# Modulation channels 5 to 8 as rows on TensorE in the mixer, x scaled during the first loads, plain first feed-forward tiles

## The chip, the cores and the metric

The kernel runs on one core of a Trainium2 chip. TensorE (PE) multiplies, VectorE (DVE), ScalarE (ACT) and GpSimd (POOL) do the element-wise work, and SyncE (SP) issues the transfers between HBM and the on-chip memory. Each engine takes its instructions in the order of one queue, and an instruction that waits holds up those behind it. The metric is device time in microseconds (us), the median of three runs.

## The reference

One layer of a diffusion backbone: a feed-forward block with half weight (FFN1), a token mixer of two parallel groups (gated linear attention, GLA, and a chunked gMLP), a second feed-forward block (FFN2) and a final RMSNorm. It has 1024 latent tokens, 256 context tokens, width 1024, hidden width 2816. Nine modulation channels of 1024 numbers each come from the conditioning vectors: `m_x` for the latents, `m_c` for the context.

```python
def adaln(cond, w, b):                       # w: (1024, 9 * 1024)
    return (jax.nn.silu(cond) @ w + b).reshape(cond.shape[0], ADA_MODS, 1, D_MODEL)

x = x + 0.5 * m_x[:, 2] * swiglu(modulate(rmsnorm(x, norm1_g), m_x[:, 0], m_x[:, 1]), ff1_in, ff1_out)
h = h + 0.5 * m_c[:, 2] * swiglu(modulate(rmsnorm(h, norm1_g), m_c[:, 0], m_c[:, 1]), ff1_in, ff1_out)
y_x = modulate(rmsnorm(x, norm2_g), m_x[:, 3], m_x[:, 4])          # and y_c from h
...                                          # projections, 3x3 grid convolution, GLA scans, gMLP
x = x + m_x[:, 5] * mix_x
x = x + 0.5 * m_x[:, 8] * swiglu(modulate(rmsnorm(x, norm3_g), m_x[:, 6], m_x[:, 7]), ff2_in, ff2_out)
return rmsnorm(x, final_g)
```

Channels 5 to 8 are needed for the latents only: 5 scales the mixer's output, 6 and 7 are the shift and scale in front of FFN2, 8 scales its output.

## The kernel before, in words

Activations are kept transposed: 8 tiles of 128 channels (index `k` or `dt`), and tokens in blocks of 512, 512 (`tb` 0 and 1) and 256 (`tb` 2, the context). A product to full precision is three matmuls, high part by high part, high by low and low by high, for each of its K tiles; the weights' halves `wh`/`wl` (`gh`, `gl`, `vh`, `sh`, ... in the FFNs) come from a `raw` tile by an ACT copy and a subtraction on POOL or DVE.

The FFNs work on 22 hidden tiles. For each, the two 512-token blocks and the two halves of K are combined in the Strassen-Winograd manner: seven products of 12 matmuls with 512 columns instead of eight (84 instead of 96). `winograd` orders the products of a hidden tile 1, 2 | 5, 7, 6 | 3, 4, and puts 1 and 2 of the next tile ahead of 3 and 4 (`first`). FFN1 also has 48 matmuls of 256 columns per hidden tile for the context (`gc`). The right operands (`hl`, seven sums or differences of normalized x, in two halves) are made once per FFN by `right_ops`, on DVE and ACT.

Modulation is computed in two ways. Channels 0 and 1 as rows on PE (`ada_first`): silu(c), two columns wide, is the stationary operand; each 128x1024 tile of the weights `wa` moves through; the 2x512 sums are copied by ACT (`row`, L214) and turned into columns by small matmuls (`cols`, L216). The other seven as dot products on DVE (`ada_part`): for each of 8 tiles and 2 halves a 256 KB load `ar<-in_wb` and an instruction `junk<-ar,cr` (L169) that multiplies by a broadcast silu(c) and accumulates along the row. Channels 2 to 4 (96 loads in the source, both conditions) run in FFN1, 5 to 7 (48 instructions, behind the GLA output of block 1) while the mixer ends, and 8 (16) in FFN2.

The order is not the source's. A scheduler simulates the engines, takes ready instructions by priority, and writes one queue for each engine; `after(a, b)` fixes an order by hand. Tiles come from pools with a set number of buffers by tag: `raw` 2, `ar` 2, `w` 6, `m` 8, `d` 32, `h` 7, PSUM banks `pg` and `po` 3 each, `pn` 2. A load into a pool waits until the last reader of the buffer's previous tile is done. `load` puts a 512 KB piece into `raw` unless a tag is given.

In the mixer, `mixer_front` projects K, then the four value tiles ("v tiles", `z` by L357, L359, L360: 60 matmuls), evacuates them by ACT (`acc`, `ct`, L813), convolves them on DVE (L791) and transposes them (`tr`, L841), then the two query tiles. At the mixer's end `wo_half`/`wo_add` multiply with the output projection; DVE adds to x (L1372), and x comes back from HBM (`x<-xd`, L1317).

Of the kernel before, what the change touches and what calls it, by code (L numbers as in the profile page):

```python
# [26 lines left out]
class Layer:  # L27
# [150 lines left out]
    def cond_row(self, j, c, dst):  # L178

        nc = self.nc  # L180
        n = c.stop - c.start
        t = self.tile(self.sb, 512, "ar", "cv")[:, :n] if n <= 512 else dst
        nc.sync.dma_start(t, self.a["cvec"][j:j + 1, c].to_broadcast([P, n]))
        nc.scalar.activation(dst, t, AF.Silu)
# [18 lines left out]
    def ada_rows(self, src, pr, i):  # L203
        wt = self.load(src[i], tag="d")
        for h in range(2):
            self.nc.tensor.matmul(pr[h][:2], self.sc[:, i, :], wt[:, h * 512:h * 512 + 512],  # L206
                                  start=(i == 0), stop=(i == NK - 1))

    def ada_cols(self, ch, pr):
        nc = self.nc  # L210
        row = self.m("row")
        pt = self.po("cols")
        for h in range(2):
            nc.scalar.activation(row[:2, h * 512:h * 512 + 512], pr[h][:2], AF.Copy)  # L214
            for dt in range(4 * h, 4 * h + 4):
                nc.tensor.matmul(pt[:, 2 * dt:2 * dt + 2], row[:2, dt * P:(dt + 1) * P], self.ident[:2, :2],  # L216
                                 start=True, stop=True)
        self.ada_bias(ch, 2, pt[:, :2 * NK].rearrange("p (k j) -> p k j", j=2))

    def ada_first(self):  # L220

        pr = [[self.po("row") for _ in range(2)], [self.pg("row") for _ in range(2)]]
        for i in range(NK):
            for ch in range(2):
                self.ada_rows(self.a["wa"][ch], pr[ch], i)
        for ch in (1, 0):
            self.ada_cols(ch, pr[ch])
# [56 lines left out]
    def spread(self, y, nt):  # L284

        nc = self.nc
        bc = self.pn("bc")
        for t in range(nt):
            nc.tensor.matmul(bc[:, t * P:(t + 1) * P], y[:, t:t + 1].to_broadcast([P, P]), self.ident,
                             start=True, stop=True)  # L290
        return bc
# [154 lines left out]

    def right_ops(self, tb, coef, bc, mov):
# [3 lines left out]
        for k in (0, 4, 1, 5, 2, 6, 3, 7):  # L451
# [4 lines left out]
        def out(i, b, k):  # L456
            t = self.hl(b)
            mov[i][k] = t[:, :512], t[:, 512:]

        for k in range(4):  # L460
            if tb == 0:
                out(1, self.x[k][0], k)
                out(2, self.x[k + 4][0], k)
            else:
                (b11, b12), (b21, b22) = self.x[k][:2], self.x[k + 4][:2]
                self.combos(b11, b12, b21, b22, lambda i, b: out(i, b, k))
# [14 lines left out]
    def winograd(self, jobs):  # L481
# [24 lines left out]

        first(0)
        for j, job in enumerate(jobs):
# [11 lines left out]
    def ffn(self, mov, yc, w1, w2, gates, load_x, load_c, tail, done, after_out=None):  # L520
# [14 lines left out]
        def plain(ps, parts, moving):  # L535

            n = len(parts)
            for i, ((hi, lo, c), (mh, ml)) in enumerate(zip(parts, moving)):
                nc.tensor.matmul(ps, hi[:, c], mh, start=i == 0, stop=False)  # L539
                nc.tensor.matmul(ps, hi[:, c], ml, start=False, stop=False)  # L540
                nc.tensor.matmul(ps, lo[:, c], mh, start=False, stop=i == n - 1)  # L541

        class Hidden:
# [3 lines left out]
            def ctx(s, i):  # L547
                w = s.w()
                rows = [(*w[r], slice(k * P, k * P + P)) for r in ((1, 2), (0, 4))[i] for k in range(4)]
# [3 lines left out]
                plain(ps, rows, yc)  # L553
# [9 lines left out]
                nc.sync.dma_start(hc[s.f // 2, :, h:h + 512], o.bitcast(F32))  # L563

# [51 lines left out]
        for f in range(NF):  # L616
            w = lazy(w1[f], nc.vector)
            jobs.append((w, 0, mov, Hidden(f, w)))
# [9 lines left out]
        class Out:  # L628
# [4 lines left out]
            def ctx(s):  # L633
                w = s.w()
                ps = layer.po("oc")
                for i in range(2):
                    rows = [(*w[r], slice(s.col + k * P, s.col + k * P + P)) for r in ((1, 2), (0, 4))[i]
                            for k in range(s.kd)]
                    plain(ps[:, i * 256:i * 256 + 256], rows, s.right()["ctx"])
# [62 lines left out]
        def last():  # L702
# [3 lines left out]
                     for i in range(2)]  # L706
            rows = lambda w, i, col: [(*w[r], slice(col + k * P, col + k * P + P)) for r in ((1, 2), (0, 4))[i]
                                      for k in range(kd)]
            for tb in range(2):
# [6 lines left out]
                for m, i, w, col in tiles:  # L716
                    dt = m + 4 * i
                    ps = self.po("o") if i else self.pg("o")
                    plain(ps, rows(w, i, col), right)
# [8 lines left out]
            if yc:  # L728
# [6 lines left out]
                for m, i, w, col in tiles:  # L735
# [4 lines left out]
                    plain(ps, rows(w, i, col), right)  # L740
# [33 lines left out]
        self.winograd(jobs)  # L774
# [188 lines left out]
    def mixer_front(self, y):  # L963
# [356 lines left out]
    def mixer(self, y, done=None):  # L1320
# [8 lines left out]
        row = self.d("cr")  # L1329
        self.cond_row(0, slice(0, 1024), row)  # L1330
        for ch in (5, 6, 7):
            for h in range(2):
                for dt in range(NK):
# [210 lines left out]
```

## Time and profile before

| | us |
|---|---|
| median of 3 runs | 2159.13 (2155.48 to 2160.04) |
| the profiled execution | 2155.53 |
| its span, first to last instruction | 2153.8 |
| PE busy, DVE busy | 2015.6, 1503.2 |
| mean granted clock of PE | 0.968 of 2.4 GHz |

In the span's order: the start up to about 130 us, FFN1 to about 860, the mixer's front to 1094, GLA and gMLP to 1316, the output projection to about 1452, FFN2 to the end. A row of a timeline gives start and duration in us, the engine, the line of the kernel, what is written from what, how many instructions it groups, and in brackets the idle time of the engine before it with its releaser. Durations of pipelined matmuls overlap: twelve of 512 columns stand in 2.88 us though each has 0.39.

### The profile page before, as it was taken

What the parts mean: (1) busy time and instruction counts of PE and PEld (TensorE: products, weight loads), DVE (VectorE), ACT (ScalarE), POOL (GpSimd) and SP (SyncE); (2) the same over time, 40 slices, a digit from 0 to 9 for tenths busy, and PEclk for the clock granted to TensorE, in tenths of its full rate; (3) what the DMA queues carried; (4) which work ended last, traced back from release to release, by engine and by line L of the source; (5) the groups of instructions that cost most, each with busy time, mean ns of one, the idle gap of its engine ahead of it and who ended that gap; (6) DMA issues with size and microseconds to landing.
All of it is one profiled execution on the core that took longest, in us unless ns stands there. A gap on an engine that the chain in (4) does not pass through costs nothing.

```text
span 2153.8 us, 28445 instructions
## 1 busy us (share of the span) xinstructions
PE 2015.6 (94%) x10868; PEld 1669.6 (78%) x10868; DVE 1503.2 (70%) x2503; ACT 816.5 (38%) x1297; POOL 379.9 (18%) x215
## 2 busy tenths in 40 slices
PE   6799999999999999898999998787999999999997
PEld 1678888888887888787788877565888888868875
DVE  3976665656655779869888377778677786755585
ACT  3643333333333121256456345325343444442111
POOL 0000000000025555223210010300000000065740
PEclk9799999999999999999999899897999999999998
DMA  7033333333368786321111126550444343458742
GB/s 286 25 127 118 123 142 118 122 118 118 118 222 340 275 295 240 147 79 54 49 56 50 35 91 219 200 183 28 166 158 165 112 181 137 182 216 350 306 143 79
DMA packets 111273, 332.27 MB, mean 154 GB/s; under 512 B 12448, under 2 KB 15392, under 8 KB 111136
## 3 DMA queue, kind: packets, MB, share of 16 engines
q1 hardware_dynamic: 111136, 330.45, 41.8%
q8 instruction: 85, 1.39, 0.3%
q14 instruction: 52, 0.43, 0.1%
HBM read 231.31 MB, written 99.09 MB: 153 GB/s over the span
## 4 chain that ended last, share of the span: by engine, by line
PE 72%; DVE 18%; DMA 5%; issue 2%; ACT 2%; POOL 0%; SPq 0%; DVEq 0%; ACTq 0%
PE c L492 14%; PE a L492 14%; PE f L492 14%; PE b L492 7%; DVE acc L791 3%; DMA ar<-in_wb 2%; PE gc L541 2%; PE gc L540 2%; PE gc L539 2%; PE row L206 1%; DVE hl L444 1%; PE o L541 1%; PE o L539 1%; PE o L540 1%; DVE junk L169 1%
## 5 line engine op out<-in xcount | busy, mean ns | idle before, releaser
L384 POOL TENSOR_TENSOR s<-raw 128x512 f32<-128x512 f32 x18 | 23.8, 1322 | 1149.0 <-DVE ch L526 602.0
L169 DVE SCALAR_TENSOR_TENSOR junk<-ar,cr 128x512 bf16<-128x512 f32 x160 | 112.5, 703 | 58.6 <-DMA ar<-in_wb 44.1
L390 ACT ACTIVATE gh<-raw 128x1024 fp32r<-128x1024 f32 x62 | 65.7, 1059 | 171.6 <-PE c L492 64.1
L492 PE MATMUL f<-hl,uh 128*128 128x512 f32 x528 | 126.8, 389 | 0.0
L443 ACT ACTIVATE hl<-g 128x512 fp32r<-128x512 f32 x106 | 64.3, 626 | 157.4 <-DVE g L526 153.0
L492 PE MATMUL a<-hl,gh 128*128 128x512 f32 x352 | 114.4, 403 | 8.8 <-ACT hl L443 6.3
L492 PE MATMUL c<-hl,sh 128*128 128x512 f32 x352 | 111.1, 393 | 11.7 <-ACT hl L443 9.6
L394 ACT ACTIVATE sh<-s 128x1024 fp32r<-128x1024 f32 x62 | 65.5, 1057 | 147.1 <-PE a L492 87.1
L492 PEld LDWEIGHTS f<-hl,uh 128*128 128x128 f32 x528 | 99.1, 188 | 20.6
L492 PE MATMUL b<-hl,gh 128*128 128x512 f32 x352 | 112.3, 396 | 0.8 <-ACT hl L443 0.8
L492 PE MATMUL a<-hl,sh 128*128 128x512 f32 x352 | 110.1, 393 | 1.0 <-ACT g L567 1.0
L492 PE MATMUL f<-hl,th 128*128 128x512 f32 x352 | 110.2, 390 | 0.8 <-ACT hl L443 0.8
L492 PE MATMUL c<-hl,th 128*128 128x512 f32 x352 | 108.9, 391 | 0.0
L526 DVE TENSOR_TENSOR u<-c,u 128x512 f32<-128x512 f32 x44 | 30.2, 687 | 109.0 <-ACT u L577 109.0
L791 DVE SCALAR_TENSOR_TENSOR acc<-z,par,acc 128x945 f32<-128x945 f32 (+2 forms) x64 | 93.1, 1477 | 11.6 <-ACT acc L813 10.5
L143 POOL TENSOR_TENSOR wl<-raw,wh 128x1024 fp32r<-128x1024 f32 x20 | 52.0, 2606 | 257.5 <-ACT wh L142 257.2
L444 DVE TENSOR_TENSOR hl<-g,hl 128x512 fp32r<-128x512 f32 x106 | 74.9, 724 | 26.1 <-ACT hl L443 26.0
L492 PEld LDWEIGHTS c<-hl,sh 128*128 128x128 f32 x352 | 66.4, 189 | 27.4 <-ACT hl L443 10.2
L385 DVE TENSOR_TENSOR sl<-s,sh 128x1024 fp32r<-128x1024 f32 x44 | 54.8, 1246 | 45.2 <-PE gc L540 21.9
L492 PEld LDWEIGHTS a<-hl,gh 128*128 128x128 f32 x352 | 67.1, 195 | 23.0 <-ACT hl L443 6.8
L492 PEld LDWEIGHTS b<-hl,gh 128*128 128x128 f32 x352 | 67.3, 191 | 15.8 <-ACT hl L443 1.8
L492 PEld LDWEIGHTS a<-hl,sh 128*128 128x128 f32 x352 | 66.6, 189 | 15.7 <-ACT g L567 1.3
(342 smaller groups left out, 6030.6 us busy)
## 6 DMA issues: line engine op xcount, KB each, us to landing
hd<-hl SPq DMA_DIRECT2D x142, 512.0 KB, 3.6
hc<-hd SPq DMA_DIRECT2D x142, 512.0 KB, 7.4
ar<-in_wb SPq DMA_DIRECT2D x112, 256.0 KB, 3.1
raw<-in_ff1i SPq DMA_DIRECT2D x44, 512.0 KB, 3.7
raw<-in_ff2i SPq DMA_DIRECT2D x44, 512.0 KB, 4.5
raw<-in_ff1o SPq DMA_DIRECT2D x22, 512.0 KB, 4.9
raw<-in_ff2o SPq DMA_DIRECT2D x22, 512.0 KB, 4.8
x<-in_xT SPq DMA_DIRECT2D x16, 512.0 KB, 6.8
```

The lines of the kernel that those rows point to most:

```text
L143: eng.tensor_tensor(out=lo[:, :n], in0=src[:, :n], in1=hi[:, :n].bitcast(F32), op=ALU.subtract)
L169: i = nc.vector.scalar_tensor_tensor(out=self.junk, in0=w, scalar=1.0, in1=cbc[j], op0=ALU.mult, op1=ALU.mult, accum_out=acc[:, h, dt, j:j ...
L385: sub = lambda o, x, y: eng.tensor_tensor(out=o, in0=x, in1=y, op=ALU.subtract)
L390: nc.scalar.activation(gh, g, AF.Copy)
L394: nc.scalar.activation(sh, s, AF.Copy)
L443: nc.scalar.activation(t[:, :512], src, AF.Copy)
L444: nc.vector.tensor_tensor(out=t[:, 512:], in0=src, in1=t[:, :512].bitcast(F32), op=ALU.subtract)
L492: mm = lambda x, y, start, stop: nc.tensor.matmul(ps, x, y, start=start, stop=stop, skip_group_check=more)
L539: nc.tensor.matmul(ps, hi[:, c], mh, start=i == 0, stop=False)
L540: nc.tensor.matmul(ps, hi[:, c], ml, start=False, stop=False)
L541: nc.tensor.matmul(ps, lo[:, c], mh, start=False, stop=i == n - 1)
L791: self.nc.vector.scalar_tensor_tensor(out=o, in0=zv[:, r0 + dr:r1 + dr, c0 + dc:c1 + dc], scalar=self.par[:, tap:tap + 1], in1=o, op0=ALU. ...
```

## The change

At the start, x and the weights `w0` of FFN1's first hidden tile are loaded ahead of the 16 pieces of `wa`. One set of statistics covers all three blocks, and x is multiplied by its 1/rms on DVE as soon as that is spread; channels 0 and 1 then need only a scale and a shift on ACT (`shift`). The row matmuls of channels 0 and 1 stand behind the spread, in four column groups of PE: the sums of the four 512-wide halves lie on PSUM partitions 0, 32, 64 and 96 of one bank. `right_ops` forms the operands in another order.

The first hidden tile of each FFN is computed without Winograd: block 0 (48 matmuls) ahead of products 1 and 2 of the second tile, block 1 (48) behind them. FFN2's `w0` is loaded between the two halves of the output projection (`weights2`).

Channels 5 to 8 are computed as rows on PE (`ada_steps`): per channel eight `load`s of 512 KB into `raw`, two row matmuls each, four ACT copies, eight small matmuls with a selection matrix. One channel follows each v tile in `mixer_front`. The 48 + 16 `junk` instructions with their `ar` loads go.

```diff
+    def ada_first(self, order):
+        pr = self.pg("row")
+        wts = [[self.load(self.a["wa"][ch, i], tag="d") for ch in range(2)] for i in range(NK)]
+        mm, order = order()
...
+                    g = 32 * (2 * ch + h)
+                    self.after(mm, nc.tensor.matmul(pr[g:g + 2], self.sc[:, i, :], wts[i][ch][:, h * 512:h * 512 + 512],
+                                                    start=(i == 0), stop=(i == NK - 1)))
...
+    def ada_steps(self, chs):
...
+        for i, ch in chs:
+            pr = self.pn("row")
+            for k in range(0, NK, 2):
+                wts = [self.load(self.a["wa"][i, k + e]) for e in range(2)]
+                for e in range(2):
+                    for h in range(2):
+                        g = 64 * e + 32 * h
+                        nc.tensor.matmul(pr[g:g + 2], self.sc[:, k + e, :], wts[e][:, h * 512:h * 512 + 512],
+                                         start=(k == 0), stop=(k == NK - 2))
+                if k == NK - 2:
+                    row = self.h("row")
+                    nc.vector.memset(row, 0.0)
+                    for g in range(0, P, 32):
+                        nc.scalar.activation(row[g:g + 2], pr[g:g + 2], AF.Copy)
+                    pt = self.po("cols")
+                    for dt in range(NK):
+                        nc.tensor.matmul(pt[:, 2 * dt:2 * dt + 2], row[:, dt % 4 * P:dt % 4 * P + P], sel[:, dt // 4],
+                                         start=True, stop=True)
+                    self.ada_bias(ch, 2, pt[:, :2 * NK].rearrange("p (k j) -> p k j", j=2))
+                yield
...
+    def shift(self, x, coef, k, j=0):
+        A, B = coef
+        self.nc.scalar.activation(x, x, AF.Identity, scale=A[:, k, j:j + 1], bias=B[:, k, j:j + 1])
...
+        plain.block0()
         first(0)
+        plain.block1()
...
+        ada = self.ada_steps([(2, 5), (3, 6), (4, 7), (5, 8)])
         for h in range(4):
             ct = self.h("ct")
             t = self.qkv_tile(y, a["wi"][2 + h], 4 + h, None, ct[:, :256])
+            for _ in range(4):
+                next(ada)
...
-        row = self.d("cr")
-        self.cond_row(0, slice(0, 1024), row)
-        for ch in (5, 6, 7):
-            for h in range(2):
-                for dt in range(NK):
-                    self.ada_part(ch, dt, h, [row[:, h * 512:h * 512 + 512]])
...
+        weights()
         ws = []
...
+            bc, mm = self.spread(r[:, 4 * tb:4 * tb + n // P], n // P, True)
+            for k in range(NK):
+                i = nc.vector.tensor_tensor(out=self.x[k][tb], in0=self.x[k][tb], in1=bc[:, :n], op=ALU.mult)
...
-                 done2b, self.ada_todo((8,), 1, 1, 16))
+                 done2b)
```

PE's queue before, at the end of the first v tile (`z_8440`, `z_8467`, `z_8494` are its three blocks, `z_8560` begins the next; `tr` are transposes of a K tile):

```order
L360 MATMUL z_8494<-y_7670,wl_8435 128x256
L357 MATMUL z_8494<-y_7670,wh_8434 128x256
L359 MATMUL z_8494<-y_7672,wh_8434 128x256
L360 MATMUL z_8494<-y_7670,wl_8435 128x256
L841 MATMUL tr_8415<-ident,acc_8317 128x128 [waits Activation_49]
L841 MATMUL tr_8415<-ident,acc_8317 128x128 x3
L357 MATMUL z_8560<-y_7268,wh_8554 128x512 [waits Activation_49]
```

PE's queue after, at the end of the first v tile (`z_8348`) and the beginning of the second (`z_8468`):

```order
L391 MATMUL z_8348<-y_7646,wl_8289 128x256
L246 MATMUL row_8392<-raw_8393,sc 2x512 [waits DMAHW6_49]
L246 MATMUL row_8392<-raw_8393,sc 2x512
L246 MATMUL row_8392<-raw_8395,sc 2x512 [waits DMAHW1_49]
...
L246 MATMUL row_8392<-raw_8419,sc 2x512 [waits DMAHW7_49]
L246 MATMUL row_8392<-raw_8419,sc 2x512
L255 MATMUL cols_8431<-sel,row_8425 128x2 [waits DVE_49,Activation_49]
L255 MATMUL cols_8431<-sel,row_8425 128x2 x7
L973 MATMUL tr_8443<-ident,acc_8293 128x128 [waits DVE_49]
L973 MATMUL tr_8443<-ident,acc_8293 128x128 x3
L973 MATMUL tr_8449<-ident,acc_8293 128x128 x4
L388 MATMUL z_8468<-y_7244,wh_8462 128x512 [waits Activation_49]
```

Between the two z tiles stand 16 row matmuls, each pair behind a load of its own, and the cols matmuls behind ACT. With the other three v tiles one pair stands early in the next z tile and 14 at its end.

SP's queue after, the loads of the same channel and the weights of the second v tile (`raw_8460`):

```order
L132 DMA raw_8393<-in_wa 128x1024 [waits DMAHW6_49,DMAHW2_49,Pool_49]
L132 DMA raw_8395<-in_wa 128x1024 [waits DMAHW3_49,Pool_49]
L132 DMA raw_8401<-in_wa 128x1024 [waits DMAHW6_49,PE_49]
L132 DMA raw_8403<-in_wa 128x1024 [waits DMAHW1_49,PE_49]
L132 DMA raw_8409<-in_wa 128x1024 [waits DMAHW4_49,DMAHW2_49,PE_49]
L132 DMA raw_8411<-in_wa 128x1024 [waits DMAHW5_49,DMAHW3_49,PE_49]
L132 DMA raw_8417<-in_wa 128x1024 [waits DMAHW4_49,PE_49]
L132 DMA raw_8419<-in_wa 128x1024 [waits DMAHW7_49,DMAHW5_49,PE_49]
L132 DMA raw_8460<-in_wi 128x1024 [waits DMAHW6_49,DMAHW0_49,PE_49]
```

Before, the `in_wi` loads of the v tiles followed one another in this place, each waiting for POOL. Now the third load and those behind it wait for PE.

## Rows read from the trace of the kernel before

**Rows 1.** The page's first part and the chain that ended last, by engine.

```profile
PE 2015.6 (94%) x10868; PEld 1669.6 (78%) x10868; DVE 1503.2 (70%) x2503; ACT 816.5 (38%) x1297; POOL 379.9 (18%) x215
...
PE 72%; DVE 18%; DMA 5%; issue 2%; ACT 2%; POOL 0%; SPq 0%; DVEq 0%; ACTq 0%
```

**Rows 2.** Timeline of PE at the start (columns as told above).

```profile
16.27 25.91 PE L206 MATMUL row<-raw,sc 128*2 128x512 f32 x60
42.11 3.73 PE L216 MATMUL cols<-ident,row 2*128 2x2 f32 x32
```

**Rows 3.** Timelines of ACT and of DVE at the start.

```profile
41.36 2.02 ACT L214 ACTIVATE row<-row 2x512 f32<-2x512 f32 x4 [6.05 <-PE row L206]
...
48.16 0.17 DVE L231 SCALAR_TENSOR_TENSOR A<-mods,par 128x16 f32<-128x16 f32 x1
```

**Rows 4.** Windows: stretch, its us, busy us of each engine, clock, DMA share, GB/s.

```profile
46.00:63.00 17.00, 4.95 (x21) 4.60 (x21) 15.38 (x40) 8.47 (x17) 0.00 (x0) 0.50 0.19 63
63.00:129.00 66.00, 52.49 (x254) 43.14 (x255) 58.74 (x109) 40.24 (x70) 0.00 (x0) 0.87 0.12 40
```

**Rows 5.** Timeline of PE, the first rows of the third and fourth hidden tiles.

```profile
128.67 0.62 PE L492 MATMUL a<-hl,gh 128*128 128x512 f32 x2
...
153.36 0.28 PE L541 MATMUL gc<-y,uh 128*128 128x256 f32 x1
153.48 0.63 PE L492 MATMUL a<-hl,gh 128*128 128x512 f32 x2
```

**Rows 6.** Timelines of ACT and of PE in the mixer's front.

```profile
1023.97 0.53 ACT L813 ACTIVATE ct<-z,par 128x256 f32<-128x256 f32 x1
...
1072.26 0.47 ACT L813 ACTIVATE ct<-z,par 128x256 f32<-128x256 f32 x1
...
1021.36 0.50 PE L357 MATMUL z<-y,wh 128*128 128x512 f32 x1 [3.14 <-ACT acc L813]
```

**Rows 7.** Windows of the mixer's front and of what follows it.

```profile
1016.00:1032.00 16.00, 12.58 (x54) 10.36 (x55) 14.76 (x20) 14.00 (x30) 2.68 (x1) 0.89 0.23 66
1094.00:1316.00 222.00, 214.42 (x2181) 182.24 (x2181) 145.37 (x279) 115.94 (x198) 29.06 (x14) 0.95 0.24 80
```

**Rows 8.** Waits of PE from 1316 to 1530: total us, times, longest.

```profile
PE wo L357 <- DVE x L1372: 19.5, 13, 11.6
```

**Rows 9.** Windows of the output projection and of FFN2's start.

```profile
1316.00:1341.00 25.00, 21.25 (x185) 16.97 (x184) 21.41 (x55) 5.62 (x9) 1.06 (x1) 0.94 0.48 161
1341.00:1355.00 14.00, 2.54 (x22) 2.27 (x20) 6.66 (x15) 4.41 (x5) 0.23 (x1) 0.69 1.01 388
1355.00:1455.00 100.00, 87.33 (x364) 67.64 (x364) 78.45 (x156) 26.68 (x42) 16.20 (x9) 0.98 0.52 172
1455.00:1483.00 28.00, 16.63 (x52) 12.89 (x53) 23.82 (x48) 18.44 (x32) 0.00 (x0) 0.63 0.14 47
1483.00:1515.00 32.00, 28.46 (x110) 20.95 (x109) 25.00 (x39) 16.45 (x26) 0.00 (x0) 0.95 0.06 17
```

**Rows 10.** Timelines of SP and of DVE in the output projection.

```profile
1316.32 16.17 SPq L167 DMA_DIRECT2D ar<-in_wb  x6
...
1399.35 0.69 DVE L169 SCALAR_TENSOR_TENSOR junk<-ar,cr 128x512 bf16<-128x512 f32 x1 [0.88 <-DMA ar<-in_wb]
...
1402.79 0.69 DVE L169 SCALAR_TENSOR_TENSOR junk<-ar,cr 128x512 bf16<-128x512 f32 x1 [0.93 <-DMA ar<-in_wb]
```

**Rows 11.** Timeline of PE in FFN2's first tiles.

```profile
1511.41 2.88 PE L492 MATMUL f<-hl,uh 128*128 128x512 f32 x12
...
1515.04 0.62 PE L492 MATMUL a<-hl,gh 128*128 128x512 f32 x2
```

**Rows 12.** Timeline of PE in the mixer: four transposes, 48 half-width passes.

```profile
1192.24 0.60 PE L841 MATMUL tr<-ident,kd 128*128 128x128 f32 x4
...
1193.23 2.84 PE L1055 MATMUL ds<-v,kt 128*64 128x128 f32 x48
```

**Rows 13.** The page's DMA issues: KB each, median us to landing.

```profile
raw<-in_wi SPq DMA_DIRECT2D x16, 512.0 KB, 3.5
```

More of the change, by code (lines that the diff above doesn't have):

```diff
@@ L282, in rstd_cols, with spread @@
         return y
-    def spread(self, y, nt):
+    def spread(self, y, nt, last=False):
         nc = self.nc
@@ L533, in ffn, with plain, rows @@
         pairs0 = NF // 2 - CHUNKS[-1]
-        def plain(ps, parts, moving):
+        def plain(ps, parts, moving, more=False):
             n = len(parts)
+            mm = lambda x, y, a, b: nc.tensor.matmul(ps, x, y, start=a, stop=b, skip_group_check=more)
             for i, ((hi, lo, c), (mh, ml)) in enumerate(zip(parts, moving)):
-                nc.tensor.matmul(ps, hi[:, c], mh, start=i == 0, stop=False)
-                nc.tensor.matmul(ps, hi[:, c], ml, start=False, stop=False)
-                nc.tensor.matmul(ps, lo[:, c], mh, start=False, stop=i == n - 1)
+                mm(hi[:, c], mh, i == 0 and not more, False)
+                mm(hi[:, c], ml, False, False)
+                mm(lo[:, c], mh, False, i == n - 1)
+        def rows(w, rs):
+            return [(*w[r], slice(k * P, k * P + P)) for r in rs for k in range(4)]
         class Hidden:
@@ L552, in ctx @@
                 ps = s.pc[:, i * 256:i * 256 + 256]
-                plain(ps, rows, yc)
+                plain(ps, rows(w, ((1, 2), (0, 4))[i]), yc)
                 if i == 0:
@@ L615, in ffn @@
         jobs = []
-        for f in range(NF):
-            w = lazy(w1[f], nc.vector)
+        for f in range(1, NF):
+            w = lazy(w1[f], nc.vector, self.m if f == 1 else None)
             jobs.append((w, 0, mov, Hidden(f, w)))
@@ L718, in last @@
                     ps = self.po("o") if i else self.pg("o")
-                    plain(ps, rows(w, i, col), right)
+                    plain(ps, parts(w, i, col), right)
                     more(self.x[dt][tb], ps, dt, 0)
@@ L739, in last @@
                     ps = pc[:, i * 256:i * 256 + 256]
-                    plain(ps, rows(w, i, col), right)
+                    plain(ps, parts(w, i, col), right)
                     more(self.x[dt][2], ps, dt, 1)
@@ L1387, in run @@
+        self.ada_first(scaled)
+        self.alloc_y(y, 2)
         c1 = self.norm_coef(0, C_N1, 2, "1")
         mov = {i: [None] * 4 for i in range(1, 8)}
-        self.right_ops(0, c1, self.spread(rs[0], 4), mov)
-        y = ({}, {})
-        self.alloc_y(y, 2)
-        self.norm(part(2), c1, y, rs[2])
-        self.right_ops(1, c1, self.spread(rs[1], 4), mov)
+        for k in range(NK):
+            hi, lo = y[0][2][k], y[1][2][k]
+            x = self.x[k][2]
+            self.shift(x, c1, k, 1)
+            nc.scalar.activation(hi, x, AF.Copy)
+            nc.vector.tensor_tensor(out=lo, in0=x, in1=hi.bitcast(F32), op=ALU.subtract)
```

212 lines of the change are left out of this document (158 added, 54 removed).

## The prediction

> **What bounds the kernel now.** I read the page first. TensorE (PE) is busy 94% of the span and is 72% of the chain that ended last; DVE has 18%, DMA 5% [rows 1]. So a gain or loss counts only where PE is idle, cold, or made to wait. I then took the four stretches that the change touches, each by the windows and the timeline of PE and of the engine PE waits for.
>
> Start: PE puts 60 of its 64 thin row passes into 25.91 us, 0.43 us each, and is done with the cols matmuls near 45.8 [rows 2]; the coefficient A of the first norm starts at 48.16 on DVE [rows 3]. From 46 to 63 PE is busy 4.95 of 17 us, at a granted clock of 0.50 (the 1.2 GHz level); from 63 to 129 it has 52.49 of 66 and DVE 58.74, so DVE paces the first products [rows 4]. The products of the third hidden tile begin at 128.67, those of the next at 153.48; from there on the start no longer matters [rows 5].
>
> Mixer front: the context part of a v tile is evacuated first at 1023.97 and last, for the fourth, at 1072.26, 16.1 us apart on the mean; one gap of PE there is 3.14 us, for ACT's `acc` [rows 6]. Behind the stage (1094 to 1316) PE has 214.42 of 222 us, so a delay in it is not made good later [rows 7].
>
> Output projection (wo): PE waits 13 times for DVE's addition to x, 19.5 us in all, once 11.6 [rows 8]. From 1316 to 1455 PE has 21.25 + 2.54 + 87.33 = 111.1 of 139 us [rows 9]. What keeps DVE: `junk`, the modulation products, each of which waits for its 256 KB; SP spends 16.17 us on six such issues from 1316.32, and what is queued behind them waits too [rows 10].
>
> FFN2's start: PE 16.63 of 28 us at clock 0.63, then 28.46 of 32, while DVE works 23.82 and 25.00 [rows 9]; the third tile's products begin at 1515.04 [rows 11].
>
> **The change part by part**, against the profiled execution: 2155.53 us, span 2153.8, 3.6 below the median 2159.13.
>
> *Start.* x and the first tile's weights now load ahead of the 16 wa loads; all statistics and x times rstd run under those loads. The last wa is the 28th load of 0.524 MB; at 388 GB/s, which a stretch of full queues shows [rows 9], 1.35 us each, so it lands near 41 us, and the next tile's weights, on which a DVE difference waits that stands ahead of the row copy, near 43. The row passes now lie in four column groups of one bank. Nearest row: `ds` puts 48 passes of 128 columns, in two groups, into 2.84 us, 58 ns each, where four full-width transposes of as many columns take 0.60 us, about 110 each with the last one's tail taken off [rows 12]. So two groups overlap nearly twofold; four groups of 512 columns no row shows: between 27.3 us (64 by 0.43, no overlap) and a quarter, 7. The loads hide most of it: rows end at 41 to 51. The copies (4 in 2.02 us [rows 3]), cols and bias follow: coefficients at about 53, against 48.16. But then only one ACT pass stands before the first right operand, not statistics, rstd, spread and a DVE product for each of 16 x tiles (0.69 us by the nearest such instruction [rows 10]: 11 us off a DVE that is busy 58.74 of 66). Work up to the mark: 144 matmuls by 0.227 (12 in 2.88 us, less the last one's 0.39, over 11 steps [rows 11]) = 32.7; 96 of 256 columns by 0.12 [rows 5] = 11.5; 12 more for the plain tile = 2.7; together 46.9. Begun at about 59 that ends at 106 without a stall; with 7 us of waits and cold matmuls (before: 66 us for 44.2, so 22) at 113: **-16** (-24 with no stall and early rows, -6 if rows end at 51 and ACT paces).
>
> *Plain first tiles* cost 12 by 0.227 = 2.7 us each and are in the marks above and below.
>
> *Channels 5 to 8 as rows.* Per v tile the order puts 16 row matmuls (32 passes) in a run behind z. Each waits for its `raw`, each raw's load for PE's release of the one two back, since the ring has two buffers, and the next v tile's own weights are queued on SP behind these eight. Two of the eight can load while z runs. The other six go three times around the ring: a load L, and PE's use r of one raw (four passes). L: 512 KB of in_wi take 3.5 us alone [rows 13]; with two in flight I take 3.6. r: 1.7 serial (4 by 0.43), 0.43 if four groups overlap fully; I take 1.1, near the twofold of rows 12. The run is 3L + 5r = 10.8 + 5.5 = 16.3 us (12.7 to 19.3). Then PE waits for 4 ACT copies (2.02 us [rows 3]) and does 8 cols matmuls, 16 passes by 0.117 (32 in 3.73 [rows 2]) = 1.9. The next weights leave for their load one raw before the run ends and must then be split by ACT and POOL, about 1 us more than copies and cols hide. 21.2 us a channel, 85 for four, less about 2 for idle PE that it covers: **+83**. Bounds: 60, with full overlap and the copies half hidden; 112, with none, and z cold behind each run (in the stretch with the 3.14 us gap the clock is 0.89 [rows 7]). ACT's row copies stand behind a silu that waits for DVE's conv; DVE was busy 14.76 of 16 us there, in a period that now is more than twice as long, so nothing for that.
>
> This ring is judged by the nearest two-buffer ring, ar: a pair is used from 1399.35, the next from 1402.79: 3.44 us for 1.4 us of DVE work, and half the bytes [rows 10]. The Trainium skill (Trainium Kernel Development and Optimization, section Best Practices) advises to double-buffer so that DMA and compute overlap. By it the six loads would lie beside other work, which is the far end of rival B. Here the row speaks against the rule: two buffers don't overlap a load with anything when the engine that uses them has nothing else in its queue and each use is shorter than a load.
>
> *wo stage.* 48 junk instructions and their 48 loads leave it, so DVE adds to x at once and the x loads are not behind six issues. PE's idling is 139 - 111 = 28 us; 25 of it goes (the 19.5 behind x, and the waits of colder matmuls after it), and some 3 us of slower matmuls (clock 0.69 from 1341 to 1355 [rows 9]). Next late are the gate loads and the products of them: **-28** (-15 if these or the x loads keep PE waiting; -36 if wo's 384 by 0.227 = 87 us and 16 us of other work are all that is left of 139).
>
> *FFN2's start.* From 1455 to 1515.04 PE has 32.7 us of matmuls up to the mark and about 4 of statistics and takes 60; plain adds 2.7. The first 48 matmuls need only x's block 0, and their weights are loaded in the wo stage. Of the 23 us of waits and cold matmuls I take two thirds to go, 15, less 2.7: **-12** (-20 to -5). Sixteen junk instructions leave FFN2, where little PE time hangs on them: **-1** (-3 to 0).
>
> Sum: -16 + 83 - 28 - 12 - 1 = **+26**: 2181.5 by the profiled execution, 2185 as a median.
>
> **Rivals.**
> A, the forecast: the ring makes PE wait some 16 us per channel. For it: rows 10, 13 and the order.
> B, the ring is cheap: two loads in flight take hardly more than one, r is 0.43, and the copies are half hidden; the term is 60 and the four gains (57 together) come above their middle, near 75. Sum -16: 2143, faster. The side turns where the run falls below about 10 us per channel with the gains at their middle, or 14 with the gains at 75. Its far end, with all loads beside other work, is a term of 16 for copies and cols and the middle gains: -41, 2118; I give that 0.03 of B's chance. Against it: PE's queue is in order, with nothing between the rows. The Trainium skill (TensorE: Matmul & The Clock Gate, Part 3) gives 2.38 times for three column tiles of 32 by 512; by it r would be 0.7, A's run 14.4 and A's sum +18; no row here has three or four tiles.
> C, the groups don't overlap and z is cold behind each run: 105 to 112 in place of 83: sum +51, 2210. For it: 0.43 us for each thin pass at the start [rows 2] and the clock of rows 7; against it, rows 12.
> D, the wo stage keeps idling, since x and gate loads, not junk, set it: -15 there: sum +39, 2198. Against it: rows 8 and 10.
>
> **How the numbers follow.** A 0.62, B 0.20, C 0.10, D 0.08. The range goes from B's centre to a little past C's, 2142 to 2224; A alone would be 2168 to 2204. About 0.2% (4 us) can be told from no change here. Faster has most of B and a sliver of A, 0.20; within 0.2%: 0.05; slower 0.75.
>
> **What the next profile would show.** Right: PE idle before `row` some 3 us at a time, released by DMA in_wa, 8 or so times per v tile; ct evacuations 36 to 39 us apart; no junk in the wo stage and no 11 us hole in wo; the first mark near 113. Wrong, if in_wa waits are under 1 us or the evacuations stay under 30 us apart (B), or if row passes stand 0.43 us apart with z cold behind them (C), or if PE still waits for `x` in wo (D).

## The result, and the profile after

The changed kernel takes 2213.99 us (2210.72 to 2216.14) against 2157.31 us in the same session: a ratio of 1.0263, interval 1.024 to 1.0286, 57 us slower where 26 were forecast. Its profiled execution has a span of 2208.9 us, 55.1 more than before. Seven marks in PE's queue say where; the last column is for the first experiment below.

| mark, us from the span's start | before | after | after, channels 5 to 8 on DVE |
|---|---|---|---|
| first product of the third hidden tile | 128.67 | 120.18 | 120.12 |
| first z matmul of the mixer | 925.8 | 915.3 | 916.7 |
| last z matmul (its high-part form) | 1093.8 | 1177.7 | 1084.5 |
| first `ds` matmul of the context | 1165.2 | 1254.4 | 1158.5 |
| first `mix` matmul | 1315.8 | 1405.0 | 1309.7 |
| last `wo` matmul (its high-part form) | 1448.5 | 1510.9 | 1432.9 |
| span | 2153.8 | 2208.9 | 2135.0 |

Differences of neighbouring marks give the terms: start and FFN1 -10.5, mixer up to `ds` +99.7, output projection -26.8 (from `ds` to the last `wo`), all behind it -7.3; sum +55.1.

Start, PE's timeline after, answering to [rows 2, 5]:

```profile
41.91 8.71 PE L214 MATMUL row<-raw,sc 128*2 128x512 f32 x64
51.44 1.67 PE L225 MATMUL cols<-ident,row 2*128 2x2 f32 x16 [0.82 <-DVE row L222]
...
64.08 0.58 PE L637 MATMUL gc<-y,vh 128*128 128x256 f32 x1 [7.12 <-ACT y L1553]
...
72.91 0.58 PE L637 MATMUL gc<-y,vh 128*128 128x256 f32 x1 [3.10 <-ACT y L1553]
...
120.18 0.63 PE L589 MATMUL a<-hl,gh 128*128 128x512 f32 x2
```

64 thin passes now stand in 8.71 us, 0.136 each against 0.43. That still understates the overlap of the four column groups, as the first 16 passes took some 1.0 us each and the other 48 took 0.59. The row of those 48 alone:

```profile
45.27 5.35 PE L214 MATMUL row<-raw,sc 128*2 128x512 f32 x48
```

They are 0.111 us apart, 3.9 times as dense as the 0.43 of a single group. But the first context product waits 7.12 us for ACT, and another 3.10: from 56.01, where ACT begins its shifts, ACT and not PE or the rows sets the start.

Mixer, ACT's evacuations of the context part of the first and the fourth v tile, answering to [rows 6]:

```profile
1007.94 0.53 ACT L945 ACTIVATE ct<-z,par 128x256 f32<-128x256 f32 x1
...
1131.87 0.47 ACT L945 ACTIVATE ct<-z,par 128x256 f32<-128x256 f32 x1
```

They are 41.3 us apart on the mean, against 16.1. PE's timeline shows the first channel's run, from its first to its last row (not all are shown), and then the stop around the second channel:

```profile
1004.84 1.04 PE L246 MATMUL row<-raw,sc 128*2 128x512 f32 x8
...
1023.06 1.87 PE L246 MATMUL row<-raw,sc 128*2 128x512 f32 x4 [1.62 <-DMA raw<-in_wa]
...
1049.02 1.04 PE L246 MATMUL row<-raw,sc 128*2 128x512 f32 x8
1053.75 3.14 PE L246 MATMUL row<-raw,sc 128*2 128x512 f32 x8 [3.69 <-DMA raw<-in_wa]
1059.58 1.87 PE L246 MATMUL row<-raw,sc 128*2 128x512 f32 x4 [2.69 <-DMA raw<-in_wa]
1062.75 1.87 PE L246 MATMUL row<-raw,sc 128*2 128x512 f32 x4 [1.29 <-DMA raw<-in_wa]
1065.17 1.87 PE L246 MATMUL row<-raw,sc 128*2 128x512 f32 x4 [0.55 <-DMA raw<-in_wa]
1069.53 3.57 PE L255 MATMUL cols<-sel,row 128*128 128x2 f32 x16 [2.49 <-ACT row L252]
1072.96 1.95 PE L973 MATMUL tr<-ident,acc 128*128 128x128 f32 x8
1074.56 0.78 PE L388 MATMUL z<-y,wh 128*128 128x512 f32 x1
1075.13 0.63 PE L390 MATMUL z<-y,wh 128*128 128x512 f32 x1
1075.56 0.63 PE L388 MATMUL z<-y,wh 128*128 128x512 f32 x1
```

The first channel's 32 passes, eight pieces, take 20.1 us, from 1004.84 to 1024.93. In the second channel PE does 28 passes from 1049.02 to 1067.04 (the first piece's four stand at 1034.86, in the z tile before), with 8.2 us of waits for pieces. The first eight passes run in four column groups and take 1.04 us; after that the pieces come one by one, each feeds two groups only, and its four passes take 1.87 us. Then PE waits 2.49 us for ACT's copies, does the cols matmuls in 3.57 us (0.22 each, where before 32 took 3.73), eight transposes in 1.95, and begins z with matmuls 0.43 us apart or somewhat more: 25.5 us from the run's start to z's. A piece lands 3.6 us after its issue, in the median:

```profile
raw<-in_wa SPq DMA_DIRECT2D x31, 512.0 KB, 3.6
```

Windows of that stop and of the z tile behind it, answering to [rows 7], and PE's waits from 1000 to 1178 (total, times, longest):

```profile
1050.00:1073.00 23.00, 12.30 (x41) 3.94 (x37) 8.43 (x9) 4.97 (x8) 2.35 (x1) 0.55 0.52 161
1073.00:1091.00 18.00, 18.00 (x91) 14.48 (x95) 1.78 (x3) 4.17 (x8) 0.00 (x0) 0.91 0.20 58
```

```profile
PE row L246 <- DMA raw<-in_wa: 32.8, 19, 3.7
PE cols L255 <- ACT row L252: 9.9, 4, 2.5
```

The granted clock is 0.55 on the mean in the stop. Of the 99.7 us only 42.7 are waits for pieces and copies. PE's busy time from the first z to the first `ds` matmul grew from 223.48 to 289.01 us: most of the rest is PE at work, much of it at the 1.2 GHz level.

Output projection, the window that answers to [rows 9]:

```profile
1405.00:1515.00 110.00, 106.72 (x569) 89.48 (x569) 72.59 (x125) 35.98 (x54) 18.73 (x12) 0.96 0.29 92
```

PE has 106.72 of 110 us; no wait for x is left where 19.5 us stood in [rows 8]. The longest of those, 11.6 us, ended in the kernel before when DVE had channel 5, which scales what is added to x. DVE there, the coefficient and the first additions:

```profile
1353.61 0.17 DVE L155 TENSOR_TENSOR mods<-acc,par 128x8 f32<-128x8 f32 x1
...
1354.30 2.06 DVE L1372 SCALAR_TENSOR_TENSOR x<-wo,mods,x 128x512 f32<-128x512 f32 x3
```

The coefficient comes 37.8 us behind the first `mix` matmul. Now it is ready long before.

FFN2's start, PE's timeline after, answering to [rows 11], and DVE's row for the statistics that PE holds back:

```profile
1529.44 0.95 PE L297 MATMUL st<-ones,acc 128*128 128x1 f32 x8
...
1545.79 0.79 PE L637 MATMUL c<-hl,vh 128*128 128x512 f32 x1 [4.79 <-ACT hl L474]
```

```profile
1530.42 0.16 DVE L311 TENSOR_SCALAR r<-st 128x4 f32<-128x4 f32 x1 [5.16 <-PE st L297]
```

Block 1's statistics matmuls stand behind plain matmuls in PE's queue, DVE waits 5.16 us for them, and PE later 4.79 us for operands of block 1.

### The profile page after: what moved, and what is told of

It is laid out like the page before. It is cut to its first block, busy times and chain, and to the rows that moved or that the text cites. A ratio compares the mean times of both kernels' runs of the same rounds, so it can differ in the third digit from the quotient of the medians.

```text
span 2208.9 us, 28780 instructions
## 1 busy us (share of the span) xinstructions
PE 2073.0 (94%) x11168; PEld 1715.8 (78%) x11168; DVE 1423.9 (64%) x2323; ACT 823.0 (37%) x1310; POOL 386.7 (18%) x217
## 4 chain that ended last, share of the span: by engine, by line
PE 79%; DVE 10%; DMA 6%; ACT 3%; issue 2%; SPq 0%; DVEq 0%; ACTq 0%
PE a L589 13%; PE c L589 13%; PE f L589 13%; PE b L589 7%; PE gc L637 6%; PE o L637 3%; DMA raw<-in_wa 2%; PE oc L637 2%; DVE acc L625 2%; PE z L388 1%; PE z L390 1%; PE row L246 1%; PE z L391 1%; PE wo L388 1%; DMA ar<-in_wb 1%
## 5 line engine op out<-in xcount | busy, mean ns | idle before, releaser
L923 DVE SCALAR_TENSOR_TENSOR acc<-z,par,acc 128x945 f32<-128x945 f32 (+2 forms) x64 | 82.8, 1308 | 64.5 <-ACT acc L945 63.5
L589 PE MATMUL f<-hl,uh 128*128 128x512 f32 x504 | 121.1, 389 | 0.0
L589 PE MATMUL c<-hl,sh 128*128 128x512 f32 x336 | 104.3, 391 | 1.6 <-ACT u L709 1.6
L589 PE MATMUL a<-hl,gh 128*128 128x512 f32 x336 | 105.3, 393 | 0.0
L589 PE MATMUL b<-hl,gh 128*128 128x512 f32 x336 | 105.0, 392 | 0.2 <-ACT hl L474 0.2
L589 PE MATMUL f<-hl,th 128*128 128x512 f32 x336 | 103.8, 389 | 0.0
L589 PE MATMUL a<-hl,sh 128*128 128x512 f32 x336 | 103.7, 389 | 0.0
L637 PE MATMUL o<-hc,vh 128*128 128x512 f32 x256 | 80.5, 395 | 0.4 <-DVE acc L625 0.4
L169 DVE SCALAR_TENSOR_TENSOR junk<-ar,cr 128x512 bf16<-128x512 f32 x96 | 65.3, 680 | 15.3 <-DMA ar<-in_wb 14.6
L589 PEld LDWEIGHTS f<-hl,th 128*128 128x128 f32 x336 | 63.1, 188 | 13.1
```

The source lines that it names most:

```text
L169: i = nc.vector.scalar_tensor_tensor(out=self.junk, in0=w, scalar=1.0, in1=cbc[j], op0=ALU.mult, op1=ALU.mult, accum_out=acc[:, h, dt, j:j ...
L589: mm = lambda x, y, start, stop: nc.tensor.matmul(ps, x, y, start=start, stop=stop, skip_group_check=more)
L637: mm = lambda x, y, a, b: nc.tensor.matmul(ps, x, y, start=a, stop=b, skip_group_check=more)
L923: self.nc.vector.scalar_tensor_tensor(out=o, in0=zv[:, r0 + dr:r1 + dr, c0 + dc:c1 + dc], scalar=self.par[:, tap:tap + 1], in1=o, op0=ALU. ...
```

## The experiments

The theory after the result: (T) the rows' weights go round a ring of two buffers, PE's in-order queue stops for them, and behind each stop PE works at the low clock; the other terms are smaller misses. Rivals: (R1) thin passes, copies and cols are the cost by themselves; (R2) part of the loss comes from elsewhere in the change. Ratios are to the kernel before, run beside each version. In the expectations "waits for in_wa 95 us" adds the stops of PE's weight loads (62) to those of its matmuls (33); PE's own idle time is 32.8.

**e1_ada_back: channels 5 to 8 on DVE again.**

```diff
-        ada = self.ada_steps([(2, 5), (3, 6), (4, 7), (5, 8)])
...
+        for ch in (5, 6, 7):
+            for h in range(2):
+                for dt in range(NK):
+                    self.ada_part(ch, dt, h, [row[:, h * 512:h * 512 + 512]])
...
+                 done2b, self.ada_todo((8,), 1, 1, 16))
```

> The changed kernel with channels 5 to 8 as dot products on DVE again, so only the start, the plain tiles and the early weights of FFN2 are left of the change. Theory (the rows in the mixer cost about 100 us and their absence in the output projection gives 27): the first mark stays near 120, the v tiles' context evacuations are 16 us apart again, PE waits for DVE's x some 20 us in the output projection; time 2157 - 10 - 7 = 2140 (2132 to 2148). Rival (a part of the loss in the mixer comes from the start or from moved priorities and not from the rows): over 2150.

2137.84 us, ratio 0.9915 (0.9898 to 0.9931). R2 falls: what is left of the change is 20 us faster than before. By the table's last column the rows cost 95 to 96 us up to `ds` and `mix` and give back 17.3 in the output projection; another 9.5 us there come without them. PE still waits for x, half as long as in [rows 8]. Channel 5's coefficient is ready 23.9 us behind the first `mix` matmul, not 37.8, and the hole of 11.6 us is gone:

```profile
PE wo L388 <- DVE x L1504: 10.2, 6, 4.4
```

```profile
1333.65 0.16 DVE L155 TENSOR_TENSOR mods<-acc,par 128x8 f32<-128x8 f32 x1
```

**e2_two_pieces: two of eight pieces per channel are loaded, the other products are left out by reading those two again.**

```diff
-                wts = [self.load(self.a["wa"][i, k + e]) for e in range(2)]
+                if k == 0:
+                    wts = [self.load(self.a["wa"][i, k + e]) for e in range(2)]
```

> The changed kernel with two of the eight weight pieces of each of the channels 5 to 8 loaded and the other six matmul pairs reading the same two; the products of the six other pieces are left out. 16 row matmuls, copies and cols stay. Theory (the ring of two buffers makes PE wait): waits of PE for in_wa fall from 95 to under 10 us, evacuations 20 to 24 us apart instead of 41; time 2214 - 4 x 18 = 2140 (2128 to 2152). Rival (thin passes at the low clock, copies and cols are the cost): evacuations stay over 30 apart and the time over 2170.

2153.38 us (0.9978, 0.9967 to 0.999), a little over the range that T gave. Evacuations are 27.9 us apart on the mean, between the two expectations. `ds` begins at 1197.9, 39.4 us behind e1 where the full version is 95.9 behind. So the six pieces more that go round the ring cost 56.5 us: waits, and passes that come two by two and cold. 39.4 us are what passes, copies and cols cost without them, so R1 holds for that part. PE's timeline of the first channel shows it; its 32 passes in 3.62 us are 0.113 each, at a granted clock of 1.00, and the cols are cold behind the wait for copies:

```profile
1006.53 3.62 PE L247 MATMUL row<-raw,sc 128*2 128x512 f32 x32
1015.98 3.57 PE L256 MATMUL cols<-sel,row 128*128 128x2 f32 x16 [5.83 <-ACT row L253]
```

**e3_cols_late: a channel's copies and cols behind the next tile's first rows.**

```diff
                 if k == NK - 2:
+                    yield
                     row = self.h("row")
...
-            for _ in range(4):
+            for _ in range(4 if h == 0 else 5):
                 next(ada)
```

> The changed kernel with the four ACT copies and the eight cols matmuls of a channel put behind the next v tile's first row matmuls. Theory (the ring is the cost; copies and cols are 2.5 us of waiting and 3.6 us of work at the low clock per channel): the 2.5 us waits for ACT go, nothing else; time 2214 - 4 x 2.5 = 2204 (2196 to 2210). Rival (the stop behind the run is what makes PE cold and late): under 2190.

2199.72 us (1.0199, 1.0181 to 1.0216): 14 us less than the change, inside T's range. From the first z to the first `ds` matmul it is 11.9 us less: the wait for copies was worth a little more than its 9.9 us.

**e4_spread: the steps between the blocks of a z tile.**

```diff
-            t = self.qkv_tile(y, a["wi"][2 + h], 4 + h, None, ct[:, :256])
-            for _ in range(4):
+            for tb in range(3):
+                self.qkv_gemm(o, y, 4 + h, tb, ct[:, :256])
+                if tb == 2 and h < 3:
+                    o2 = self.qkv_open(a["wi"][3 + h])
                 next(ada)
+            t = self.qkv_conv(o, 4 + h, None, ct[:, :256])
+            next(ada)
+            o = o2
```

> The changed kernel with a channel's four steps of two pieces put between the blocks of a v tile (after each of three blocks, the fourth behind the conv), and the next v tile's weights asked for ahead of the last two steps; ring of two and work unchanged. Theory (loads can lie beside z if the rows stand between its blocks): waits for in_wa fall from 95 to 20 to 40 us, evacuations 24 to 28 us apart; time 2214 - 58 = 2156 (2140 to 2170). Rival (four trips of the ring, at 4.2 us each, outlast the 13.6 us of z, and the weights of the next tile come late): evacuations over 32 apart, time over 2178.

2180.51 us (1.0112, 1.0097 to 1.0127): a miss for T, 24 us too slow; evacuations 29.3 us apart lie between the two. PE's waits in the mixer's front:

```profile
PE row L246 <- DMA raw<-in_wa: 11.7, 9, 2.4
PE z L388 <- ACT wh L142: 6.5, 3, 3.2
```

With two buffers, place alone doesn't hide the loads, and z now waits for its own weights, which are queued behind pieces.

**e5_filled_waits: ten unread full matmuls behind each two pieces, in PE's waits.**

```diff
+WARM = 10
...
+                warm = self.pg("warm")
+                for _ in range(WARM):
+                    last = nc.tensor.matmul(warm, self.yw[:, :P], self.yw, start=True, stop=True)
+                    self.after(mm, last)
```

> The changed kernel with ten extra full matmuls of 512 columns (results read by nobody) behind each two weight pieces of a channel, ordered so that they fall into PE's waits for the next pieces and for the row copies. Ring, loads and the needed work as they were. Theory (part of the cost is the 1.2 GHz level behind the waits): the clock of the mixer's front rises above 0.9, the cols matmuls take 1.9 instead of 3.6 us, the next z tile starts at 0.23 us a matmul instead of 0.43; the fillers (2.3 us at the high clock, per 3.6 us of waiting) cost nothing; 2214 - 4 x 4.5 = 2196 (2188 to 2206). Rival (the clock doesn't matter here, the loads alone set the pace): fillers show as 2214 to 2235.

2185.67 us (1.013, 1.0113 to 1.0147): 28 us faster by 160 more matmuls, a little below T's range. The window of the mixer's front and a run in PE's timeline:

```profile
1001.00:1161.00 160.00, 149.32 (x728) 99.37 (x727) 58.46 (x79) 52.28 (x94) 16.65 (x7) 1.00 0.41 129
```

```profile
1047.03 2.18 PE L247 MATMUL row<-raw,sc 128*2 128x512 f32 x8
1049.14 2.60 PE L253 MATMUL warm<-y 128*128 128x512 f32 x10
1051.84 1.03 PE L247 MATMUL row<-raw,sc 128*2 128x512 f32 x4
...
1062.83 1.95 PE L262 MATMUL cols<-sel,row 128*128 128x2 f32 x16
```

The clock is 1.00; cols take 1.95 instead of 3.57 us, a piece's four passes take 1.03 instead of 1.87, and the last z matmul comes at 1161.5, 16.2 us earlier (z itself begins 1.2 us earlier, so 15 to 16). That is the price of the clock in this stage, on an unchanged ring. Another 6 us went between `ds` and `mix`, for which no run has a cause.

**e6_products_early, on e1: the products of channels 5 to 7 asked for earlier.**

```diff
+        row = self.d("cr")
+        self.cond_row(0, slice(0, 1024), row)
+        for ch in (5, 6, 7):
...
         on = [self.gla_norm(0, g0, [self.queries(0, dt) for dt in range(2)])]
...
-        for ch in (5, 6, 7):
```

> The version with channels 5 to 8 on DVE (2138), with the products of channels 5 to 7 asked for before the GLA output of block 0 instead of behind the one of block 1, where DVE is busy about half of the time. Theory (what is left of PE's waits for x in the output projection, 10 us, is the tail of those products): the last product ends before 1400 instead of at 1422, waits for x under 3 us, time 2130 (2124 to 2136). Rival (they then stand in front of DVE work that the GLA waits for): 2138 or more.

2140.1 us (0.9917, 0.9901 to 0.9934), no gain; T falls here and the rival stands. The waits for x in `wo` are gone, but `mix` begins late (duration, first and last start):

```profile
L1412 PE MATMUL mix<-wst,vs x128: 272/421/473, 1338.2 to 1353.4; 128*64 128x128 f32 x128
```

1338.2 against 1309.7 in e1: the products stood ahead of DVE work that the GLA needs. The profiled execution is the slowest of six, 2148.23 us, so some 8 us of what it shows are not in the median.

**e7_ctx_shift_dve, on e1: the context's scale and shift on DVE.**

```diff
-            self.shift(x, c1, k, 1)
+            nc.vector.tensor_scalar(out=x, in0=x, scalar1=c1[0][:, k, 1:2], scalar2=c1[1][:, k, 1:2], op0=ALU.mult,
+                                    op1=ALU.add)
```

> The version with channels 5 to 8 on DVE (2138), with the scale and shift of the context's eight tiles at the start on DVE instead of ACT. Theory (at the start ACT paces PE: it is busy without a gap from 63 to 75 us while DVE idles 7 us): ACT is rid of 8 by 0.5 us, the first context matmul at 61 instead of 64, the first mark 2 to 4 us earlier; time 2135 (2132 to 2138). Rival (the x operands behind it set the mark anyway): no difference, 2138.

2128.2 us (0.9856, 0.984 to 0.9873): 9.6 us less than e1, more than expected, and the fastest version measured.

```profile
61.69 0.58 PE L637 MATMUL gc<-y,vh 128*128 128x256 f32 x1 [5.15 <-ACT y L1557]
```

The first context product comes at 61.69 instead of 65.47, z at 911.3 instead of 916.7: 5.4 us at the start, as ACT was the pace. The rest lies behind `ds`: 3.1 us up to `mix`, 1.6 in the output projection, 2.1 in FFN2. What moved there is open; the profiled execution is the fastest of four, 2124.58 us.

**e8_ffn2_winograd, on e1: no plain tile in FFN2, its weights loaded late.**

```diff
-            late["w0"] = self.halves(a["ff2i"][0], nc.gpsimd, self.w)
+            late["w0"] = None
...
-        for f in range(1, NF):
+        for f in range(1 if w0 else 0, NF):
```

> The version with channels 5 to 8 on DVE (2138), with FFN2's first hidden tile by seven products again and its weights loaded behind the output projection as before; FFN1 keeps its plain tile. Theory (the plain tile costs 2.7 us of matmuls but gives PE work while block 1 is prepared, net 4 us won): 2142 (2138 to 2146). Rival (the statistics of block 1 stand behind plain matmuls in PE's queue, so the plain tile wins nothing): 2135 or less.

2145.95 us (0.9944, 0.9928 to 0.9959): 8 us slower than e1, the upper end of T's range. In this version the plain tile and its early weights more than earn their 2.7 us of extra matmuls. That is not a gain of 8 us over the kernel before: behind the last `wo` matmul it took 705.3 us, e1 takes 702.1, and e8 711.7. With seven products again FFN2 is 6.4 us longer than it was, and which of the other edits costs that (the operands' new order is one) no run separates. PE's waits without the tile:

```profile
PE c L589 <- ACT hl L474: 9.7, 1, 9.7
PE wo L388 <- DVE x L1506: 9.4, 9, 2.2
PE bc L320 <- DVE r L287: 5.2, 1, 5.2
```

**e9_six_buffers: the pieces of the changed kernel in the pool of six.**

```diff
-                wts = [self.load(self.a["wa"][i, k + e]) for e in range(2)]
+                wts = [self.load(self.a["wa"][i, k + e], tag="w") for e in range(2)]
```

> The changed kernel with the weight pieces of channels 5 to 8 loaded into the pool of six buffers that also holds the split weights of the z tiles, instead of the pool of two; nothing else is edited. Theory (the depth of the ring sets PE's waits): with about four pieces ahead of PE a run keeps one or two trips instead of three; waits for in_wa fall from 95 to 45 to 65 us, evacuations 33 to 36 us apart, 2214 - 28 = 2186 (2172 to 2200). Rival (the transfers themselves set the pace, or the split weights now wait for a buffer): over 2206.

2158.6 us (0.9998, 0.9987 to 1.0009): one word takes back 55 us, twice what T expected, and the loss against the kernel before with it. Against e1, which has the products on DVE, it is still 21 us behind. PE's wait for pieces and the window of the stage:

```profile
PE row L246 <- DMA raw<-in_wa: 9.3, 7, 2.8
```

```profile
1001.00:1178.00 177.00, 155.04 (x1268) 117.21 (x1268) 126.60 (x169) 83.48 (x158) 24.80 (x10) 0.95 0.36 120
```

PE waits 9.3 us instead of 32.8, at clock 0.95; evacuations are 25.9 us apart. The next z tile's weights no longer share a ring with the pieces, either; what depth gives and what this gives no run separates. `ds` begins 62.5 us earlier than in the changed kernel but `mix` only 44.0, as PE has more work between the two (169.1 us, 168.2 of them busy, in place of 150.6); another 8.5 us come in the output projection.

**e10_x_shift_dve, on e7: four of x's first shifts on DVE too.**

```diff
+                    nc.vector.tensor_scalar(out=x[kk][0], in0=x[kk][0], scalar1=A[:, kk, 0:1],
+                                            scalar2=coef[1][:, kk, 0:1], op0=ALU.mult, op1=ALU.add)
```

> The version with channels 5 to 8 and the context's shift on DVE (2128), with four of the first eight scale-and-shift instructions of x on DVE too. Theory (ACT still paces the start: PE waited 5.2 and 2.1 us for it): ACT is rid of 4 by 0.7 us, the first mark 2 us earlier: 2126 (2122 to 2129). Rival (DVE, which makes the low halves, now paces): 2128 or more.

2149.44 us (0.9954, 0.9941 to 0.9968): T's range is missed, and the rival's number came true but not its reason. z begins at 908.6, 2.7 us earlier, much as T had it, and from `mix` to the last `wo` matmul the profiled execution loses it nine times over (147.0 us against 121.6 in e7):

```profile
PE wo L388 <- DVE x L1508: 28.7, 8, 21.4
```

SP's timeline in this kernel, and in e7:

```profile
1300.38 19.68 SPq L167 DMA_DIRECT2D ar<-in_wb  x5
1320.15 1.33 SPq L1453 DMA_DIRECT2D x<-xd  x3
```

```profile
1284.92 37.18 SPq L167 DMA_DIRECT2D ar<-in_wb  x14
1322.15 1.37 SPq L1449 DMA_DIRECT2D x<-xd  x3
```

From 1250 us on 17 `ar` loads had gone ahead of the x loads in e7, here ten: the scheduler placed the products of channels 5 to 7 later, some 1200 us behind the edit. Channel 5 is sixteen of these products, and `wo`'s 21.4 us end with it, as the 11.6 us did before:

```profile
1351.74 0.16 DVE L155 TENSOR_TENSOR mods<-acc,par 128x8 f32<-128x8 f32 x1
...
1352.43 2.06 DVE L1508 SCALAR_TENSOR_TENSOR x<-wo,mods,x 128x512 f32<-128x512 f32 x3
```

The coefficient comes 51.0 us behind the first `mix` matmul here, 21.7 in e7.

**e11_six_ctx and e12_six_spread: e9 with the context's shift on DVE, and that with e4's places.**

```diff
-                wts = [self.load(self.a["wa"][i, k + e]) for e in range(2)]
+                wts = [self.load(self.a["wa"][i, k + e], tag="w") for e in range(2)]
...
-            self.shift(x, c1, k, 1)
+            nc.vector.tensor_scalar(out=x, in0=x, scalar1=c1[0][:, k, 1:2], scalar2=c1[1][:, k, 1:2], op0=ALU.mult,
+                                    op1=ALU.add)
```

In e12 also e4's edit.

> The changed kernel with six buffers for the weight pieces (2159) and the context's shift on DVE. Theory (the 5.6 us that the shift gave at the start are PE time and add to any version): 2153 (2149 to 2156). Rival (the rest of the 10 us that it gave in the version on DVE came from moved products in the output projection, which this version hasn't): no more than 6 us here; 2148 or less would speak for a cause at the start alone.

> As that one, with the row steps between the blocks of the z tiles too. Theory (what is left of PE's waits, 23 us for in_wa, goes when depth and place come together; the 32 thin passes, 3.6 us, and cols, 1.9 us, per channel stay): 2153 - 23 = 2130 (2122 to 2140), evacuations 21 to 24 us apart. Rival (the copies, the cols and the moved weights of the next tile keep it): 2145 or more.

2142.89 us (0.9926, 0.9907 to 0.9945): 16 us under e9, where 6 were expected; z begins 5.0 us earlier, the other 11 lie between `ds` and `mix`, and what moved there is open. 2135.48 us for e12 (0.9892, 0.9871 to 0.9914), inside T's range. The window of e12's mixer:

```profile
1001.00:1178.00 177.00, 169.50 (x1419) 126.60 (x1418) 120.32 (x181) 84.45 (x159) 22.97 (x10) 0.99 0.38 124
```

With depth and place together PE is busy 169.50 of 177 us, and its waits for pieces are down to 1.3 us. Rows on PE then cost their work and hardly a wait: from the first z to the first `mix` matmul e12 takes 33 us more than e7, which has the products on DVE, and PE is busy 35 us more. It gets 18 back in the output projection and 3.5 in FFN2, and ends 7 us behind e7 in the medians (11 in the profiled executions).

## Why the prediction was right and wrong

The direction and the mechanism were right: PE's queue stops for a ring of two buffers, and DVE's relief in the output projection doesn't pay for it. With two pieces in place of eight the ring's part goes (e2), and with six buffers the whole loss (e9). The size was half: +26 forecast, +55.1 between the profiled executions. Of the 29 us between them 16.7 are the rows, 5.5 the start, 1.2 the output projection and 5.7 FFN2, all to the same side.

*Channels as rows, +83 forecast, +99.7 measured: the term that failed.* Its load part and its work part were both counted at the high clock, and the low clock was left to the upper bound and to rival C. The load L was right, 3.6 us. The use r of a piece was taken at 1.1 us and took 1.87; with the clock held up it takes 1.03 (e5). The forecast's own form, 3L + 5r, gives 20.2 us with this r, and the first channel's run took 20.1 in place of 16.3. Behind the run copies took 2.5 for 2.0, cols 3.57 for 1.9, eight transposes 1.95, where e5 has them in 1.07, and z began at 0.43 us a matmul for some 2 us. e5 puts the clock's part at 15 to 16 us: nearly all of the miss. The pieces' price is 56 us (e2), the work's 39. Column groups do overlap, four of them 3.9 times at the start; so C's first half was wrong, and its second half, the cold tile behind the run, was true beside A and not instead of it. Of the signs named, waits before `row` released by in_wa came true (19 in four v tiles, fewer than 8 each); evacuations are 41.3 us apart, above the 36 to 39.

*Start, -16 forecast, -8.5 at the mark and -10.5 by z.* The working began the products at 59 and took 7 us of waits and cold matmuls from there on. They began at 64.08: the coefficients were some 3 us late, and then ACT made PE wait, 10.2 us in all, on 16 scale-and-shift instructions of x and eight of the context. The working had only one ACT pass in front of the first right operand. Its lower bound said "if rows end at 51 and ACT paces", and both happened (rows end at 50.6); e7 shows ACT's part, by taking eight of them away.

*Output projection, -28 forecast, -26.8 measured.* The size was right, the reason only in part: 9.5 us come without taking the products away (e1), 17.3 with it. What PE waited longest for was channel 5's coefficient, and in e1 that is ready earlier. What puts it there is open; the early FFN2 weights don't, as e8 has them late and keeps the gain. That the sum fits -28 is partly luck. Rival D is wrong.

*FFN2, -13 forecast, -7.3 measured.* Two misses partly cancel. The plain tile and the new order, -12, gave 3.2 (e1); the other 4.1 come with the rows, where -1 stood for the sixteen products that leave FFN2. The plain tile does cover DVE's work (8 us by e8), but the changed FFN2 without it is 6.4 us behind the kernel before, for a cause that no run separates, and the statistics of block 1 stand behind the tile in PE's queue. The working had no term for either.

*Rival B* (whose sum is -15 by its own terms, not -16) asked whether the loads could be cheap. They can, in e9 and e12, but by four more buffers and other places, not in this order. On the ring the trace first spoke against the rule of the Trainium skill (Trainium Kernel Development and Optimization, section Best Practices) that double-buffering overlaps DMA with compute: with two buffers the pieces cost 56 us. With six most of the overlap that it promises is there: 9.3 us of waits are left in e9, 1.3 in e12.

## What to carry to other kernels

Ask of each load not whether it is double-buffered, but how many of its latencies the consumer's queue sees in a row, and what else stands in that queue. Price the work behind a stall of PE at the low clock. Before moving work off an engine that makes others wait, find the one result that they wait for: here it was channel 5's coefficient, and when it came decided over up to 21 us of PE's time. And try the small edits first: the fastest version here is the one that left channels 5 to 8 on DVE and moved eight instructions from ACT to DVE at the start.

## What the runs showed of the hardware

Thin passes (2 by 512, on 128 rows) came 0.43 us apart in one column group and 0.113 apart in four, 3.8 times as dense, both at a granted clock of 1.00 (the kernel before at its start; e2, 32 passes in 3.62 us). With two groups at a time four passes took 1.03 us at a granted clock of 1.00 (e5) and 1.87 at 0.50. The Trainium skill (TensorE: Matmul & The Clock Gate, Part 3) states 2.38 times for three column tiles; three were not tried here. In a stretch of 23 us with short bursts and waits of 0.5 to 3.7 us between them PE's granted clock was 0.55 on the mean. Matmuls whose results nobody reads, put into those waits, held it at 1.00 and made the kernel 28 us faster; 15 to 16 of these lie in that stage.
